# Blockwise inverses of unit triangular matrices: the step from 16 to 32 rows in compact 32x32 squares

## The chip, the cores and the metric

The kernel runs on one NeuronCore of a Trainium2 chip. The core has a matrix engine (TensorE, "PE" in the profile, with its weight loads as "PEld"), a vector engine (VectorE, "DVE"), a scalar engine (ScalarE, "ACT"), a general engine (GpSimd, "POOL"), and a queue engine that issues most of the transfers (SyncE, "SP"). Matrix products read their operands from the on-chip memory SBUF, which has 128 partitions, and write to eight PSUM banks of 128 partitions by 512 f32 columns. The metric is the device time of one execution in microseconds, taken as the median of several runs. The profile is one further execution with the hardware profiler on.

## The reference

The reference computes two layers of a hybrid decoder for 256 tokens of width 2048, all in f32. Each layer is a token mixer followed by a SwiGLU block, with adaptive modulation and layer norms around both. The mixer of the first layer has a group of mLSTM heads and a group of 16 RWKV-7 heads; the mixer of the second has retention heads and eight gated DeltaNet heads. Two of these hold a linear recurrence with a rank-one correction:

```python
# RWKV-7, per head, one token at a time
sa = jnp.einsum('bhij,bhj->bhi', S, at)
S = S * wt[:, :, None, :] + sa[..., None] * bt[:, :, None, :] + vt[..., None] * kt[:, :, None, :]
# gated DeltaNet, per head and chunk
ut = jnp.eye(CHUNK) + jnp.where(strict, jnp.einsum('cbhtd,cbhsd->cbhts', kb, kc) * gamma, 0.0)
u = lax.linalg.triangular_solve(ut, vc * bc[..., None], left_side=True, lower=True)
```

The kernel treats both with chunks of 128 tokens: inside a chunk the corrections of all tokens follow from one triangular system, a unit triangular matrix of 128 by 128 per head and chunk. The kernel forms the inverse of that matrix and multiplies with it.

## The kernel before

The 256 tokens are two tiles of 128 partitions (NT = 2). Every large weight product is computed in a split form: the f32 weights stream in from memory, ScalarE rounds them to a "hi" part and VectorE subtracts to get the "lo" part (`split`, L750 and L751), and TensorE adds three products per block into a PSUM bank of the group "g" (`part`, L765 to L767: hi times hi, lo times hi, hi times lo). All small products of the mixers go to banks of the groups "m" (three banks) and "c" (two banks), as full f32 products. VectorE also computes the modulation rows (L686), one long instruction for each 128 columns.

The small work of the mixers is not a stage of its own: it is woven into the stream of weight products. The order on every engine is written out by a planner (class `Plan`). The program is first built once, the planner simulates all engines with a table of costs (`cost`, `matmul`, the constants `MARGINS`, `LAND`, `CROSS`, `RATE`), and it picks, on each engine, the ready instruction with the lowest priority number. The priority is the program's order plus a shift that the table `PLACES` gives for each range of instruction numbers. It also decides which buffer each tile gets. The program is then built a second time with that order imposed on each engine.

`inverses(mt, dd)` receives eight triangular matrices `mt` (four heads, two chunks) in one tile and a tile `dd` of the same size for the result. It is called six times: four times by `rwkv_heads` (one call for each batch of four heads) and twice by `gdn_group`. It works in four steps, each closing with a `yield`.

1. Diagonal blocks of 16 rows. L1048 to L1058 cut the 16x16 blocks out into a compact tile `e` (8 matrices by 16 columns) and run a recurrence of fourteen steps on VectorE, each a lane shuffle, a product and an addition. L1060 spreads the result over the full width of 128 columns with a mask of blocks (`blk`), which gives `dt`; L1064 transposes each 128x128 matrix on TensorE and L1065 copies the result to `d`. So `d` and `dt` hold the block-diagonal inverse and its transpose, with zeros elsewhere.
2. From 16 to 32 rows. L1074 multiplies the full 128x128 `mt` with every second block of columns of `d` (64 columns), L1078 masks the result to the wanted blocks (`lev`), L1081 multiplies with `dt`, L1084 adds into `d`, L1088 transposes again and L1089 copies to `dt`.
3. From 32 to 64 rows. L1097 multiplies 32x32 squares (for the two pairs of squares, each in a bank of its own), L1099 copies out, L1103 and L1105 give the new square and its transpose, L1108 and L1109 put them into `d` and `dt`.
4. From 64 to 128 rows. L1116 to L1125 do the same with 64x64 squares; only the transpose `dt` is made.

The result `dt` then goes into the products of the heads (for RWKV L1312, for DeltaNet L1710). GpSimd runs the triangular masks (L1131), the scalings for the decay weights (L1532, L1675) and a few memsets (L1330).

Of the kernel before, what the change touches and what calls it, by code (L numbers as in the profile page):

```python
# [16 lines left out]
ALU = mybir.AluOpType  # L17
# [4 lines left out]
P = 128  # L22
# [34 lines left out]
for _name, _w in [("ident", 128), ("cum", P + 1), ("tr", 128), ("ones", 128), ("sl", 128), ("tri", 32), ("diag", 16), ("blk", 8),  # L57
                  ("lev", 64), ("bones", 128), ("hsel", 2), ("freq", 64)]:
    CONS[_name] = (_n, _w)
    _n += _w  # L60
# [3 lines left out]
def constants():  # L64
# [3 lines left out]
    def put(name, a):  # L68
        o, w = CONS[name]
        c[:, o:o + w] = a  # L70
# [11 lines left out]
    put("blk", u // BASE == np.arange(P // BASE)[None])  # L82
    j = np.arange(64)
    s = j // BASE * 2 * BASE + j % BASE
    put("lev", (u // (2 * BASE) == s[None] // (2 * BASE)) & (u % (2 * BASE) >= BASE))
# [108 lines left out]
def finish(g):  # L194
# [10 lines left out]
MARGINS = {'Activation': 0.9875423830141832, 'DVE': 1.0101153058187327, 'PE': 1.014122181386299, 'Pool': 1.1973257770806474}  # L205
LAND, CROSS, RATE, SOON = 2471.8499431610267, 67.12701229691764, 396.01772112428813, 250.0
PLACES = (
# [29 lines left out]
class Plan:  # L237
# [85 lines left out]
    def cost(self, i):  # L323
# [26 lines left out]
        if e == "Pool":  # L350
            d = {"TensorScalarAffineSelect": 1100 if n == 512 else 900, "TensorTensor": 950, "TensorScalarPtr": 1200, "Memset": 610}.get(op, 100)
            return d, d
# [206 lines left out]
class Trunk:  # L559
# [475 lines left out]
    def inverses(self, mt, dd):  # L1035
# [4 lines left out]
        d, dt = dd[:, 0], dd[:, 1]  # L1040
        halves = [slice(0, 4), slice(4, 8)]
        four = lambda x: x.rearrange("p (h t) -> p h t", h=4)
# [16 lines left out]
        for hs in halves:  # L1059
            v.tensor_tensor(dt[:, hs, :].rearrange("p h (n c) -> p h n c", c=BASE), e[:, hs, :].unsqueeze(2).to_broadcast([P, 4, 8, BASE]),  # L1060
                            self.con("blk").unsqueeze(1).unsqueeze(3).to_broadcast([P, 4, 8, BASE]), ALU.mult)
            b = self.bank()
            for j in range(4):
                nc.tensor.transpose(b[:, P * j:P * j + P], dt[:, hs.start + j, :], self.ident)  # L1064
            nc.scalar.activation(d[:, hs, :], four(b[:]), AF.Copy)  # L1065
        yield
        mm = nc.tensor.matmul
        mask = self.con("lev").unsqueeze(1).to_broadcast([P, 4, 64])
        dv = d.rearrange("p h (n two b) -> p h n two b", two=2, b=BASE)
        b, p = [], []  # L1070
        for hs in halves:
            x = self.bank()
            for j in range(4):
                mm(x[:, 64 * j:64 * j + 64], mt[:, hs.start + j, :], dv[:, hs.start + j, :, 0, :], start=True, stop=True)  # L1074
            b.append(x)
        for x in b:
            p.append(self.own([P, 4, 64], "P", 2))
            v.tensor_tensor(p[-1][:], four(x[:, 0:256]), mask, ALU.mult)  # L1078
        for hs, x, y in zip(halves, b, p):
            for j in range(4):  # L1080
                mm(x[:, 256 + 64 * j:320 + 64 * j], dt[:, hs.start + j, :], y[:, j, :], start=True, stop=True)  # L1081
        for hs, x in zip(halves, b):
            o = dv[:, hs, :, 0, :]
            v.tensor_tensor(o, x[:, 256:512].rearrange("p (h n b) -> p h n b", h=4, b=BASE), o, ALU.add)  # L1084
        for hs in halves:
            x = self.bank()
            for j in range(4):
                nc.tensor.transpose(x[:, P * j:P * j + P], d[:, hs.start + j, :], self.ident)  # L1088
            nc.scalar.activation(dt[:, hs, :], four(x[:]), AF.Copy)  # L1089
# [3 lines left out]
        b = [self.bank(), self.bank()]  # L1093
        y = self.own([P, 8, 32], "P", 2)
        for h in range(8):
            for x, (ev, od) in zip(b, pairs):
                mm(x[od, 32 * h:32 * h + 32], mt[ev, h, od], d[ev, h, ev], start=True, stop=True)  # L1097
        for x, (ev, od) in zip(b, pairs):
            nc.scalar.activation(y[od], x[od, 0:256].rearrange("p (h b) -> p h b", h=8), AF.Copy)  # L1099
        for h in range(8):  # L1100
            c = slice(256 + 32 * h, 288 + 32 * h)
            for x, (ev, od) in zip(b, pairs):
                mm(x[od, c], dt[od, h, od], y[od, h, :], start=True, stop=True)  # L1103
            for x, (ev, od) in zip(b, pairs):
                mm(x[ev, c], y[od, h, :], dt[od, h, od], start=True, stop=True)  # L1105
# [882 lines left out]
```

## Time and profile before

| what | value |
|---|---|
| median of 3 runs | 2699.81 us (2694.32 to 2701.47) |
| the profiled execution | 2710.22 us, its span 2708.5 us |
| mean granted TensorE clock | 0.984 of full speed |
| TensorE busy | 2616.7 us, 97% of the span |
| VectorE busy | 2003.0 us, 74% |
| ScalarE busy | 1270.1 us, 47% |
| GpSimd busy | 87.1 us, 3% |
| instructions in the profile | 33578 |

A share of busy time is an average over stages with different limits, so the table only says where to look. In this profile the RWKV and mLSTM work of the first layer lies between about 125 and 700 us, the first SwiGLU block between about 700 and 1420 us, the DeltaNet groups between about 1420 and 1740 us, retention and the second output product up to about 2000 us, and the second SwiGLU block after that. A row that begins with a time is a single block of instructions in order of time; a row with "x" and a mean is a group over the whole span. The duration of one TensorE instruction contains its way through the array, which overlaps with the next instruction, so the distance between two starts, not the duration, is what it costs in a full queue.

### The profile page before, as it was taken

To read this page: it belongs to the slowest core of one execution; us is meant where nothing else is said; L and a number is where in the kernel's file an instruction comes from. 1 tells how busy PE (TensorE), PEld (TensorE's weight loads), DVE (VectorE), ACT (ScalarE), POOL (GpSimd) and SP (SyncE) were. 2 spreads that over 40 slices of the span, in tenths; PEclk is the share of its full clock that TensorE was granted. 3 is DMA by queue.
4 is the path that set the end of the run, shared out by engine and by line. 5 is a ranking of instruction groups with operands and counts; after the bars stand their busy time and mean duration, and the time that the engine had idled before them with its cause. 6 is when DMAs were issued, how large, how long until landed. Compare 5 with 4: busy or idle time off the path is not lost.

```text
span 2708.5 us, 33578 instructions
## 1 busy us (share of the span) xinstructions
PE 2616.7 (97%) x12906; PEld 2157.6 (80%) x12906; DVE 2003.0 (74%) x3153; ACT 1270.1 (47%) x1705; POOL 87.1 (3%) x88
## 2 busy tenths in 40 slices
PE   4799999999999999999999999999999999999997
PEld 2578877888788888888888887888788888888886
DVE  7998877888777677767778998876956664456457
ACT  2464545565644444434446654444554444443442
POOL 0000000100000000000001102000000000000000
PEclk9899998999999999999999999999999999999999
DMA  9966655665688888867856866765657775556554
GB/s 396 386 251 236 238 202 204 239 231 192 221 310 309 321 313 322 310 218 295 325 210 213 309 234 235 267 249 205 241 210 275 257 286 191 194 200 228 187 188 169
DMA packets 105659, 681.60 MB, mean 252 GB/s; under 512 B 11861, under 2 KB 15129, under 8 KB 27417
## 3 DMA queue, kind: packets, MB, share of 16 engines
q1 hardware_dynamic: 104346, 677.36, 68.3%
q8 instruction: 101, 1.65, 0.2%
q10 hardware_dynamic: 1152, 2.10, 0.2%
q14 instruction: 60, 0.49, 0.1%
HBM read 668.89 MB, written 10.52 MB: 251 GB/s over the span
## 4 chain that ended last, share of the span: by engine, by line
PE 86%; DVE 7%; DMA 4%; ACT 1%; issue 1%; POOL 0%; SPq 0%; DVEq 0%; ACTq 0%
PE g L765 26%; PE g L766 26%; PE g L767 26%; DMA raw<-ada 2%; DVE lo L751 1%; DMA a<-ada 1%; DMA y<-w_ab 1%; PE m L1010 1%; DVE raw L686 1%; ACT hi L750 1%; PE m L1290 0%; PE m L1312 0%; PE c L1468 0%; PE m L1308 0%; PE m L1321 0%
## 5 line engine op out<-in xcount | busy, mean ns | idle before, releaser
L751 DVE TENSOR_TENSOR lo<-raw,hi 128x1024 fp32r<-128x1024 f32 (+2 forms) x802 | 970.0, 1213 | 567.7 <-ACT hi L750 564.6
L750 ACT ACTIVATE hi<-raw 128x1024 fp32r<-128x1024 f32 (+2 forms) x802 | 842.6, 1053 | 1083.9 <-PE g L767 1027.0
L765 PE MATMUL g<-hi,h 128*128 128x512 f32 (+2 forms) x2312 | 901.7, 392 | 13.5 <-ACT h L829 13.1
L766 PE MATMUL g<-lo,h 128*128 128x512 f32 (+2 forms) x2312 | 902.4, 391 | 0.6 <-DVE lo L751 0.5
L767 PE MATMUL g<-hi,h 128*128 128x512 f32 (+2 forms) x2312 | 900.6, 391 | 0.0
L765 PEld LDWEIGHTS g<-hi,h 128*128 128x128 f32 x2312 | 436.0, 189 | 103.1 <-ACT h L829 14.0
L766 PEld LDWEIGHTS g<-lo,h 128*128 128x128 f32 x2312 | 436.5, 189 | 89.3 <-DVE lo L751 2.7
L767 PEld LDWEIGHTS g<-hi,h 128*128 128x128 f32 x2312 | 436.5, 189 | 88.7 <-issue 4.2
L765 PE MATMUL g<-hi,a 128*128 128x512 f32 x920 | 358.7, 392 | 0.5 <-DVE t L906 0.5
L767 PE MATMUL g<-hi,a 128*128 128x512 f32 x920 | 358.3, 390 | 0.0
L766 PE MATMUL g<-lo,a 128*128 128x512 f32 x920 | 358.2, 390 | 0.0
L765 PEld LDWEIGHTS g<-hi,a 128*128 128x128 f32 x920 | 172.4, 188 | 37.5 <-DVE t L906 1.0
L767 PEld LDWEIGHTS g<-hi,a 128*128 128x128 f32 x920 | 172.8, 188 | 35.6
L766 PEld LDWEIGHTS g<-lo,a 128*128 128x128 f32 x920 | 172.8, 188 | 35.5
L686 DVE SCALAR_TENSOR_TENSOR raw<-raw,silu_c 128x2048 f32<-128x2048 f32 x82 | 188.6, 2303 | 11.1 <-DMA raw<-ada 6.7
L686 DVE SCALAR_TENSOR_TENSOR za<-za,silu_c 128x2048 f32<-128x2048 f32 x56 | 127.9, 2284 | 1.4 <-DMA za<-ada 1.4
L686 DVE SCALAR_TENSOR_TENSOR zt<-zt,silu_c 128x2048 f32<-128x2048 f32 x38 | 86.8, 2285 | 2.1 <-DMA zt<-ada 2.1
L1675 POOL TENSOR_SCALAR s<-cons_sb,log_alpha 128x128 f32<-128x128 f32 x16 | 28.7, 1806 | 997.0 <-DVE log_alpha L1619 853.9
L1474 DVE SCALAR_TENSOR_TENSOR f<-c,cols_sb,f 128x253 f32<-128x253 f32 (+2 forms) x120 | 55.9, 477 | 4.9 <-ACT f L1471 4.1
L948 ACT ACTIVATE t<-m,affine 128x128 f32<-128x128 f32 x96 | 35.6, 467 | 4.4 <-PE m L945 2.5
L686 DVE SCALAR_TENSOR_TENSOR a<-a,silu_c 128x2048 f32<-128x2048 f32 x16 | 36.1, 2288 | 1.9 <-DMA a<-ada 1.9
L765 PE MATMUL m<-hi,h 128*128 128x512 f32 x24 | 11.2, 468 | 23.6 <-ACT h L829 23.6
(481 smaller groups left out, 2137.7 us busy)
## 6 DMA issues: line engine op xcount, KB each, us to landing
raw<-gu SPq DMA_DIRECT2D x176, 1024.0 KB, 4.8
raw<-dn SPq DMA_DIRECT2D x88, 1024.0 KB, 4.8
raw<-ada SPq DMA_DIRECT2D x82, 1024.0 KB, 5.2
raw<-w_cd SPq DMA_DIRECT2D x60, 1024.0 KB, 4.9
za<-ada SPq DMA_DIRECT2D x56, 1024.0 KB, 7.0
raw<-w_ab SPq DMA_DIRECT2D x48, 1024.0 KB, 5.1
zt<-ada SPq DMA_DIRECT2D x38, 1024.0 KB, 7.0
a<-ada SPq DMA_DIRECT2D x16, 1024.0 KB, 16.4
```

What stands on the lines that cost most here:

```text
L686: v.scalar_tensor_tensor(w[:], w[:], 1.0, self.sc[:], ALU.mult, ALU.mult, accum_out=m[:, i:i + 1])
L750: nc.scalar.activation(hi[:, :2 * n], ws, AF.Copy)
L751: nc.vector.tensor_tensor(lo[:, :2 * n], ws, hi[:, :2 * n], ALU.subtract)
L765: mm(o, ah, wh, start=start and k == 0, stop=False)
L766: mm(o, ah, wl, start=False, stop=False)
L767: mm(o, al, wh, start=False, stop=stop and k == 3)
L948: nc.scalar.activation(h32[:, j, :], b[:, P * j:P * j + P], AF.Identity, bias=self.ab[:, sub + 1, 16 + k:17 + k], scale=self.ab[:, sub + 1 ...
L1010: nc.tensor.transpose(b[:, P * k:P * k + P], gs[:, t, P * k:P * k + P], self.ident)
L1474: v.scalar_tensor_tensor(o[:, d:T], b[:, T * j:T * j + T - d], self.col(wname, 4 * (tile0 + i + j) + 3 - d), o[:, d:T], ALU.mult, ALU.add)
L1675: nc.gpsimd.tensor_scalar(L[:], sl, self.gl[:, t, 4 * g + j:4 * g + j + 1], None, ALU.mult)
```

## The change

Step 1 no longer spreads the blocks of 16 rows over 128 columns and no longer transposes on TensorE. The two blocks of each 32x32 square are put side by side in a compact tile `a` (8 matrices by 32 columns), with a mask `par` that says which of the two blocks a partition belongs to. VectorE's square transpose, which transposes each 32x32 square of its operand by itself, gives its counterpart `c`.

Step 2 works on the four diagonal 32x32 squares of each matrix: 32 products of 32x32 by 16 columns, one scalar-tensor-tensor on VectorE that masks and adds the identity part (`two`), 32 products of 32x32 by 32 columns, a copy by ScalarE, and a second square transpose by VectorE. ScalarE and VectorE place the squares into `dt` (two squares each); `d` now has only 64 columns per matrix and keeps its squares compact. GpSimd clears `dt` and `d` at the start, since they are no longer written in full.

Step 3 uses one bank for both pairs of squares, and the square that no later step reads (the one of the second pair in `d`) is no longer computed. Step 4 is unchanged but for the narrower `d`.

The constants `blk` and `lev` go, `par` and `two` come. In the planner the cost of a GpSimd memset now grows with its size, the constants are fitted anew, and the table of shifts is a new one for the changed program.

```diff
-for _name, _w in [... ("tri", 32), ("diag", 16), ("blk", 8),
-                  ("lev", 64), ("bones", 128), ("hsel", 2), ("freq", 64)]:
+for _name, _w in [... ("tri", 32), ("diag", 16), ("par", 2),
+                  ("two", 32), ("bones", 128), ("hsel", 2), ("freq", 64)]:
...
+    put("par", u % 32 // BASE == np.arange(2)[None])
+    put("two", u % 32 == c32)
...
-MARGINS = {'Activation': 0.9875423830141832, 'DVE': 1.0101153058187327, 'PE': 1.014122181386299, 'Pool': 1.1973257770806474}
-LAND, CROSS, RATE, SOON = 2471.8499431610267, 67.12701229691764, 396.01772112428813, 250.0
+MARGINS = {'Activation': 0.9876056006034423, 'DVE': 1.0058989261580051, 'PE': 1.014, 'Pool': 1.2193352478552955}
+LAND, CROSS, RATE, SOON = 2470.0, 66.83757847790392, 395.92384460318044, 250.0
 PLACES = (
...
-        d, dt = dd[:, 0], dd[:, 1]
+        room = dd[:].rearrange("p a h t -> p (a h t)")
+        eight = lambda x: x.rearrange("p (h t) -> p h t", h=8)
+        dt, d, yi, a = eight(room[:, 0:1024]), eight(room[:, 1024:1536]), eight(room[:, 1536:1792]), eight(room[:, 1792:2048])
...
+        nc.gpsimd.memset(room[:, 0:1536], 0.0)
+        nc.scalar.activation(yi[:, :, BASE:], two[:, BASE:].unsqueeze(1).to_broadcast([P, 8, BASE]), AF.Copy)
...
-        for hs in halves:
-            v.tensor_tensor(dt[:, hs, :]..., e[:, hs, :]..., self.con("blk")..., ALU.mult)
-            b = self.bank()
-            for j in range(4):
-                nc.tensor.transpose(b[:, P * j:P * j + P], dt[:, hs.start + j, :], self.ident)
-            nc.scalar.activation(d[:, hs, :], four(b[:]), AF.Copy)
+        v.tensor_tensor(a.rearrange("p h (n c) -> p h n c", n=2), e[:].unsqueeze(2).to_broadcast([P, 8, 2, BASE]),
+                        par.unsqueeze(1).unsqueeze(3).to_broadcast([P, 8, 2, BASE]), ALU.mult)
+        c = self.own([P, 8, 32], "P", 2)
+        v.transpose(c[:], a)
         yield
...
+        quarters = [slice(32 * q, 32 * q + 32) for q in range(4)]
+        x = self.bank()
+        for h in range(8):
+            for r in quarters:
+                mm(x[r, BASE * h:BASE * h + BASE], mt[r, h, r], c[r, h, 0:BASE], start=True, stop=True)
+        v.scalar_tensor_tensor(yi[:, :, 0:BASE], eight(x[:, 0:8 * BASE]), par[:, 1:2], two[:, 0:BASE].unsqueeze(1).to_broadcast([P, 8, BASE]),
+                               ALU.mult, ALU.add)
+        for h in range(8):
+            for r in quarters:
+                mm(x[r, T + 32 * h:T + 32 * h + 32], yi[r, h, :], a[r, h, :], start=True, stop=True)
+        z = eight(x[:, T:2 * T])
+        c = self.own([P, 8, 32], "P", 2)
+        nc.scalar.activation(c[:], z, AF.Copy)
+        v.transpose(d[:, :, 0:32], c[:])
+        for q in (1, 3, 0, 2):
+            r = quarters[q]
+            if q % 2:
+                nc.scalar.activation(dt[r, :, r], z[r], AF.Copy)
+            else:
+                v.tensor_copy(dt[r, :, r], c[r])
+        v.tensor_copy(d[32:64, :, 32:64], d[32:64, :, 0:32])
         yield
...
-        b = [self.bank(), self.bank()]
+        x = self.bank()
...
-            for x, (ev, od) in zip(b, pairs):
-                mm(x[od, c], dt[od, h, od], y[od, h, :], start=True, stop=True)
+            for ev, od in pairs[:1]:
+                mm(x[od, o], dt[od, h, od], y[od, h, :], start=True, stop=True)
...
-            v.tensor_copy(d[od, :, ev], z[od])
+        for ev, od in pairs[:1]:
+            v.tensor_copy(d[od, :, 0:32], eight(x[od, T:2 * T]))
```

More of the change, by code (lines that the diff above doesn't have):

```diff
@@ L56 @@
 _n = 0
-for _name, _w in [("ident", 128), ("cum", P + 1), ("tr", 128), ("ones", 128), ("sl", 128), ("tri", 32), ("diag", 16), ("blk", 8),
-                  ("lev", 64), ("bones", 128), ("hsel", 2), ("freq", 64)]:
+for _name, _w in [("ident", 128), ("cum", P + 1), ("tr", 128), ("ones", 128), ("sl", 128), ("tri", 32), ("diag", 16), ("par", 2),
+                  ("two", 32), ("bones", 128), ("hsel", 2), ("freq", 64)]:
     CONS[_name] = (_n, _w)
@@ L81, in constants @@
     put("diag", u % BASE == c16)
[L82 to L85, printed above, removed]
+    put("par", u % 32 // BASE == np.arange(2)[None])
+    put("two", u % 32 == c32)
     put("bones", u // 64 == t // 64)
@@ L350, in cost @@
         if e == "Pool":
-            d = {"TensorScalarAffineSelect": 1100 if n == 512 else 900, "TensorTensor": 950, "TensorScalarPtr": 1200, "Memset": 610}.get(op, 100)
+            d = {"TensorScalarAffineSelect": 1100 if n == 512 else 900, "TensorTensor": 950, "TensorScalarPtr": 1200, "Memset": 610 + 0.5 * n if n > 256 else 610}.get(op, 100)
             return d, d
@@ L1039, in inverses @@
         nc, v = self.nc, self.nc.vector
-        d, dt = dd[:, 0], dd[:, 1]
+        room = dd[:].rearrange("p a h t -> p (a h t)")
+        eight = lambda x: x.rearrange("p (h t) -> p h t", h=8)
+        dt, d, yi, a = eight(room[:, 0:1024]), eight(room[:, 1024:1536]), eight(room[:, 1536:1792]), eight(room[:, 1792:2048])
         halves = [slice(0, 4), slice(4, 8)]
+        par, two = self.con("par"), self.con("two")
+        nc.gpsimd.memset(room[:, 0:1536], 0.0)
+        nc.scalar.activation(yi[:, :, BASE:], two[:, BASE:].unsqueeze(1).to_broadcast([P, 8, BASE]), AF.Copy)
         four = lambda x: x.rearrange("p (h t) -> p h t", h=4)
@@ L1058, in inverses @@
                 v.tensor_tensor(e[:, :, k + 1:], e[:, :, k + 1:], x, ALU.add)
-        for hs in halves:
-            v.tensor_tensor(dt[:, hs, :].rearrange("p h (n c) -> p h n c", c=BASE), e[:, hs, :].unsqueeze(2).to_broadcast([P, 4, 8, BASE]),
-                            self.con("blk").unsqueeze(1).unsqueeze(3).to_broadcast([P, 4, 8, BASE]), ALU.mult)
-            b = self.bank()
-            for j in range(4):
-                nc.tensor.transpose(b[:, P * j:P * j + P], dt[:, hs.start + j, :], self.ident)
-            nc.scalar.activation(d[:, hs, :], four(b[:]), AF.Copy)
+        v.tensor_tensor(a.rearrange("p h (n c) -> p h n c", n=2), e[:].unsqueeze(2).to_broadcast([P, 8, 2, BASE]),
+                        par.unsqueeze(1).unsqueeze(3).to_broadcast([P, 8, 2, BASE]), ALU.mult)
@@ L1066, in inverses @@
+        c = self.own([P, 8, 32], "P", 2)
+        v.transpose(c[:], a)
         yield
         mm = nc.tensor.matmul
[L1068 to L1089, printed above, removed]
+        quarters = [slice(32 * q, 32 * q + 32) for q in range(4)]
[3 more added lines that the diff above has]
+                mm(x[r, BASE * h:BASE * h + BASE], mt[r, h, r], c[r, h, 0:BASE], start=True, stop=True)
@@ L1095, in inverses @@
         for h in range(8):
-            for x, (ev, od) in zip(b, pairs):
-                mm(x[od, 32 * h:32 * h + 32], mt[ev, h, od], d[ev, h, ev], start=True, stop=True)
-        for x, (ev, od) in zip(b, pairs):
-            nc.scalar.activation(y[od], x[od, 0:256].rearrange("p (h b) -> p h b", h=8), AF.Copy)
+            for ev, od in pairs:
+                mm(x[od, 32 * h:32 * h + 32], mt[ev, h, od], d[ev, h, 0:32], start=True, stop=True)
+        for ev, od in pairs:
+            nc.scalar.activation(y[od], eight(x[od, 0:T]), AF.Copy)
@@ L1100, in inverses @@
         for h in range(8):
[L1101 to L1105, printed above, removed]
-        for x, (ev, od) in zip(b, pairs):
-            z = x[:, 256:512].rearrange("p (h b) -> p h b", h=8)
-            v.tensor_copy(d[od, :, ev], z[od])
-            nc.scalar.activation(dt[ev, :, od], z[ev], AF.Copy)
+            o = slice(T + 32 * h, T + 32 * h + 32)
@@ L1110, in inverses @@
+            for ev, od in pairs[:1]:
+                mm(x[od, o], dt[od, h, od], y[od, h, :], start=True, stop=True)
+            for ev, od in pairs:
+                mm(x[ev, o], y[od, h, :], dt[od, h, od], start=True, stop=True)
+        for ev, od in pairs[:1]:
+            v.tensor_copy(d[od, :, 0:32], eight(x[od, T:2 * T]))
+        for ev, od in pairs:
+            nc.scalar.activation(dt[ev, :, od], eight(x[ev, T:2 * T]), AF.Copy)
         yield
@@ L1115, in inverses @@
             for j in range(4):
-                mm(x[64:, 64 * j:64 * j + 64], mt[:64, hs.start + j, 64:], d[:64, hs.start + j, :64], start=True, stop=True)
+                mm(x[64:, 64 * j:64 * j + 64], mt[:64, hs.start + j, 64:], d[:64, hs.start + j, :], start=True, stop=True)
             b.append(x)
```

50 rows, old and new, of the table PLACES are left out of this document.

## The prediction

> **What bounds the kernel now.** I read the profile's first page before anything else, for the busy shares, the granted clock and the shares of the chain that ended last.
>
> ```profile
> span 2708.5 us, 33578 instructions
> PE 2616.7 (97%) x12906; PEld 2157.6 (80%) x12906; DVE 2003.0 (74%) x3153; ACT 1270.1 (47%) x1705; POOL 87.1 (3%) x88
> ...
> PEclk9899998999999999999999999999999999999999
> ...
> PE 86%; DVE 7%; DMA 4%; ACT 1%; issue 1%; POOL 0%; SPq 0%; DVEq 0%; ACTq 0%
> ```
>
> TensorE is busy 97% of the span and is 86% of the chain. Next comes the table of stretches, cut at the stages; its columns are the stretch, its length, then the busy time (and instructions) of PE, weight loads, VectorE, ScalarE and GpSimd, the granted clock, and the DMA share. The four inverses of the RWKV heads lie in the first row, the two of the DeltaNet groups in the third.
>
> ```profile
> 125.00:700.00 575.00, 564.92 (x3250) 459.36 (x3249) 482.33 (x1112) 318.49 (x550) 41.48 (x47) 0.96 0.63 227
> 700.00:1420.00 720.00, 719.83 (x3225) 595.11 (x3224) 519.32 (x541) 313.22 (x334) 0.00 (x0) 1.00 0.77 287
> 1420.00:1740.00 320.00, 314.40 (x1894) 265.10 (x1893) 281.47 (x598) 176.34 (x289) 38.54 (x28) 1.00 0.68 250
> ```
>
> In both mixer stages TensorE idles under 2% (10.1 of 575 us, 5.6 of 320 us), because weight products fill the gaps between the small steps. VectorE has 93 us and 39 us to spare there, and ScalarE more. So a microsecond of TensorE work taken out of an inverse should come off the time, and a shorter latency of the same inverse should not, except through the few waits left. The list of waits for the inverse's late steps confirms that these waits are small (us in total, times, longest):
>
> ```profile
> PE m L1116 <- DVE a L1108: 0.6, 2, 0.4
> PE m L1123 <- ACT P L1120: 0.6, 2, 0.3
> ```
>
> **What is removed on TensorE.** The chain of waits (start, us, what) through the second inverse gives each block's share of the path, free of the overlap that the instruction times contain. An f32 product leaves two records, so x16 is eight products; a transpose leaves one, so x4 is four.
>
> ```profile
> 314.53 0.44 PE m L1064 x4
> ...
> 315.20 0.44 PE m L1064 x4
> ...
> 315.87 1.78 PE m L1074 x16
> ...
> 319.50 0.84 PE m L1081 x8
> ...
> 321.09 0.84 PE m L1081 x8
> 321.93 0.44 PE m L1088 x4
> ...
> 325.31 0.44 PE m L1088 x4
> 325.74 0.62 PE m L1097 x32
> ...
> 328.39 0.43 PE g L767
> 328.81 0.23 PE g L765
> ```
>
> The two rounds of eight transposes (L1064, L1088) cost 4 x 0.44 = 1.76 us, the two rounds of eight 128-row products (L1074, L1081) 1.78 + 2 x 0.84 = 3.46 us. Together 5.22 us per inverse, 31.3 us for six.
>
> **What is added on TensorE.** Two rounds of 32 products of 32 rows by 32 columns (moving width 16, then 32), eight heads in four squares on the diagonal. The trace of before has no round on four diagonal squares, so I bound it by its neighbours, from the order in time of TensorE. The first three rows are the block of L1103 and L1105 that alternates over four squares; the last two are a block on one square (its partner had no bank yet).
>
> ```profile
> 327.56 0.22 PE L1103 MATMUL m<-P,y 32*32 32x32 f32 x2
> ...
> 328.20 0.19 PE L1105 MATMUL m<-y,P 32*32 32x32 f32 x1
> 328.32 0.50 PE L767 MATMUL g<-hi,h 128*128 128x512 f32 x1
> ...
> 235.29 0.69 PE L1097 MATMUL m<-y,a 32*32 32x32 f32 x16
> 235.91 0.49 PE L765 MATMUL g<-hi,h 128*128 128x512 f32 x1
> ```
>
> Four squares: 32 products (64 records) from 327.56 to 328.32, 0.76 us. One square: eight products from 235.29 to 235.91, 0.62 us, up to 78 ns each. Two squares (the L1097 x32 row above): 16 in 0.62 us. So the time goes with the products per square, eight in all three, and four squares overlap. The new rounds also have eight per square, so I take 0.76 us for each; the width of 16 may save a little, which I leave out. The return to full-size products costs 0.43 - 0.23 = 0.20 us (L767 against L765). Each round is 0.96 us, the pair 1.92 us. If nothing overlapped, a round would be 4 x 0.62 = 2.48 us, plus 0.20: the upper bound, 5.36 us for the pair. The lower bound is a pair without the return cost, 1.52 us.
>
> A rule speaks against the lower price. The Trainium skill, page "TensorE: Matmul & The Clock Gate", section "Wait — 56ns, not 53.3ns?", says that matmul starts are never closer than about 25 ns, however narrow the operand. By it 64 records would take 1.6 us, and the estimated gain of six inverses would be 6 x (5.22 - 3.6) = 9.7 us. The trace disagrees: 64 records start within 0.76 us, 12 ns apart.
>
> **The third step** (blocks of 32 into 64) loses the eight products of L1103 for the second pair. They ran beside the others at eight per square, so they are worth nothing by the same rule of rows. But it now uses one PSUM bank for both pairs, so a pair can't be held back for a bank as at 235.29 in the first inverse, where the two pairs ran one after the other. Merged, one round of 0.62 us and its return of 0.20 us go away there, and about as much in L1103/L1105; I take 1.1 us for the whole kernel, between 0 and 1.6.
>
> **TensorE in sum:** 6 x (5.22 - 1.92) + 1.1 = 20.9 us less.
>
> **The other engines.** Groups by line, shape kept apart (busy us, mean ns), and for the start of the recurrence and the first use of the result the summary of one line (min/median/max ns, first and last start):
>
> ```profile
> L1078 DVE TENSOR_TENSOR P<-m,cons_sb 128x256 f32<-128x256 f32 x12 | 4.6, 413 | 0.0
> L1056 DVE STREAM_SHUFFLE e<-e 128x112 f32<-128x112 f32 x6 | 1.8, 297 | 0.0
> L1685 DVE SCALAR_TENSOR_TENSOR a<-m,v,t 128x128 f32<-128x128 f32 x16 | 4.8, 341 | 0.1
> L1108 DVE COPY y<-m 32x256 f32<-32x256 f32 x8 | 3.4, 424 | 2.2 <-issue 2.0
> L1065 ACT ACTIVATE y<-m 128x512 f32<-128x512 f32 x8 | 4.6, 595 | 7.3 <-PE m L1064 7.2
> L1099 ACT ACTIVATE P<-m 32x256 f32<-32x256 f32 x12 | 4.5, 377 | 0.4 <-PE m L1097 0.2
> L1330 POOL MEMSET s<- 128x256 f32 x4 | 1.2, 312 | 24.5 <-DVE e L1058 14.1 <-DVE e L1056 10.4
> ...
> L1048 DVE TENSOR_TENSOR s<-a,cons_sb x24: 402/417/1301, 182.3 to 1676.7; 32x256 f32<-32x256 f32 x24
> L1060 DVE TENSOR_TENSOR y<-e,cons_sb x8: 681/684/689, 222.6 to 505.7; 128x512 f32<-128x512 f32 x8
> ```
>
> VectorE loses two masks of 512 columns (2 x 0.684), two of 256 (2 x 0.413), two additions of 256 (the same size, 2 x 0.413) and one copy (0.424): 3.44 us. It gains one mask of 256 (0.413), one scalar-tensor-tensor of 128 (0.341), three copies of 256 columns (at most 0.424 each, 1.27) and two square transposes of 256 columns. The trace has no such transpose. The shuffle is the nearest row, since it too moves lanes: 0.297 us for 112 columns, so between 0.41 (a plain 256-column pass) and 0.68 (the shuffle scaled by columns). I take 0.45, near the plain pass. Sum 2.92, a saving of 0.5 us per inverse; at 0.68 it is nothing. ScalarE loses four copies of 512 columns (2.38 us) and gains four of at most 0.377 (1.51). Neither engine sets the end, so I count zero; what hides them is the full TensorE queue. Without that cover they would still be a small gain.
>
> GpSimd gets a memset of 1536 columns. From 0.312 us at 256 columns, 1.9 us at most by scaling. It stands ahead of the recurrence, whose first instruction starts at 182.3 us while the result is first used at 222.6: some 40 us hide it. Behind it in GpSimd's queue stand the triangular masks of the heads and the scalings for the mLSTM weights; GpSimd is busy 3% of the span. The tile it clears must now be free 40 us earlier than before; the two earlier tiles of that pool belong to a batch that is finished by then. Zero.
>
> **The sum.** The profiled execution took 2710.2 us (span 2708.5 and 1.7 around it); on it the change gives 2710.2 - 20.9 = 2689. That execution lies 10.4 us above the median of 2699.8, so against the median I expect 2699.8 - 20.9 = **2679 us**. The new shifts reorder everything, and I put no gain or loss of their own in the sum. About 0.3%, 8 us, is what a measurement here can tell from no change.
>
> **Rivals.** The first is the granted clock. Rows of the table of stretches around the second and third inverse (seventh number after the length: the clock):
>
> ```profile
> 332.30:335.72 3.42, 3.42 (x38) 3.09 (x38) 3.35 (x6) 2.52 (x7) 0.00 (x0) 1.00 0.22 53
> 335.72:339.13 3.41, 3.41 (x16) 3.15 (x16) 1.61 (x7) 0.60 (x2) 0.00 (x0) 0.55 0.73 293
> ...
> 345.96:349.37 3.41, 3.41 (x17) 3.19 (x15) 0.42 (x1) 0.62 (x2) 0.00 (x0) 0.50 0.62 262
> 349.37:352.78 3.41, 3.41 (x21) 2.56 (x20) 0.42 (x1) 1.06 (x4) 0.00 (x0) 0.95 0.00 0
> ```
>
> Right after the small products the clock falls to a half from about 336 to 349.5 us, though the queue is full. At half clock, 14 us do the work of 7, so such a stretch costs some 7 us. (a) **Slower:** the two new rounds use small corners of the array and call up one more such stretch behind each of the six inverses: 6 x 7 = 42 us, against a gain of 21, gives 2721. It decides from the third new stretch on, and from the fifth the kernel is slower by more than 0.3%. Against it: 0.76 us is short, and full products stand on both sides. (b) **Faster still:** the new order loses two such stretches, 14 us: 2665. The same page of the Trainium skill, section "HAM oscillation — how this bites in real kernels", puts the fall down to idle gaps over about 3.4 us. By that (a) can't happen. The trace disagrees here: TensorE is busy 3.42 of 3.42 us in the stretch just before the fall.
>
> (c) **The squares don't overlap:** the upper bound of 5.36 us per pair leaves 6 x (5.22 - 5.36) + 1.1 = 0.3 us: 2700, no change. For it only that products of one square don't overlap; against it the four-square block. (d) **The freed time isn't filled:** the chain through VectorE takes over the mixer stages and products come late. Then half or all of the gain is lost: 2690 to 2700. For it VectorE's 84% and 88%; against it TensorE's 15.7 us of idle time in both stages. (e) **The change doesn't do what it says:** the order searched anew is worse elsewhere. If the 15.7 us double and one half-clock stretch of 7 us is added, 2679 + 23 = 2702; the order can also be better and save about half of the idle time: 2671.
>
> **How the numbers follow.** Forecast 0.47 (own range 2670 to 2688); (a) 0.06; (b) 0.15; (c) 0.07; (d) 0.13; (e) worse 0.06, better 0.06. Faster by over 0.3% (below 2692): 0.47 + 0.15 + 0.06 + 0.05 of (d) = 0.73. Slower by over 0.3% (above 2708): (a) and somewhat under half of (e) for orders worse than priced, 0.09. The rest, 0.18, is no change. The range runs from 2660, below (b), to 2703, past (e); outside lie (a) and the tails, under 0.2.
>
> **What would show it.** Right: TensorE shows 6 x (-16 - 32 + 128 - 16) = 384 more records (16 transposes and 16 products removed, 64 small products added and 8 removed per inverse), yet its busy time falls by about 21 us; the new rounds take 0.7 to 0.8 us with heads and squares alternating; TensorE's idle share stays at 3%. Wrong: rounds of over 1.5 us (c); more idle time ahead of products, put down to VectorE (d); more or fewer rows at clock 0.5 between 125 and 700 us (a, b); a gain in stages without inverses (e).

## The result and the profile after

The changed kernel takes **2675.12 us** (median of 4 runs, 2674.08 to 2677.11) against 2700.64 us of the kernel before on the same chip (4 runs, 2694.32 to 2705.73). The ratio is 0.9908, with a 95% interval of 0.9886 to 0.9929: about 25 us, or 0.9%, faster. The prediction was 2679 us. Its profiled execution took 2674.08 us, that of before 2710.22 us, and these 36 us are more than the medians differ by. The reason is the granted clock, as will be seen.

First the page of the changed kernel: the span, the busy shares, the clock in 40 slices, and the shares of the chain that ended last.

```profile
span 2672.3 us, 34350 instructions
...
PE 2580.0 (97%) x13290; PEld 2114.3 (79%) x13290; DVE 1992.2 (75%) x3153; ACT 1264.4 (47%) x1705; POOL 96.0 (4%) x94
...
PEclk9899999999999999999999999999999999999999
...
PE 81%; DVE 11%; DMA 4%; issue 2%; ACT 1%; POOL 0%; SPq 0%; DVEq 0%; POOLq 0%; ACTq 0%
```

TensorE has 13290 records, 384 more than before, and is busy 36.7 us less. It is still the bound at 97%. Next the table of stretches of the changed kernel, for the two mixer stages with inverses (columns as in the prediction: the stretch, its length, PE, weight loads, VectorE, ScalarE, GpSimd, then the granted clock, the DMA share and GB/s).

```profile
125.00:700.00 575.00, 563.70 (x3646) 448.53 (x3645) 491.52 (x1153) 331.58 (x580) 48.67 (x51) 1.00 0.65 236
...
1420.00:1740.00 320.00, 315.92 (x2058) 264.54 (x2057) 285.73 (x578) 173.32 (x274) 38.55 (x30) 0.99 0.71 264
```

TensorE idles 11.3 and 4.1 us there, 15.4 together, against 15.7 before: in these stages the freed time was filled. In the first SwiGLU block, between 700 and 1420 us, TensorE is busy 717.83 of 720 us where it was busy 719.83 before; a wait of 2.2 us for ScalarE is new there. And the clock of the first stretch went from 0.96 to 1.00. The order in time of TensorE around the new rounds of the first inverse (start, duration, line, operands, and x records):

```profile
226.88 0.39 PE L765 MATMUL g<-hi,h 128*128 128x512 f32 x1
227.19 0.73 PE L1072 MATMUL m<-P,a 32*32 32x16 f32 x64
227.85 0.50 PE L763 MATMUL g<-hi,h 128*128 128x512 f32 x1
228.19 0.39 PE L764 MATMUL g<-lo,h 128*128 128x512 f32 x1
...
231.29 0.75 PE L1077 MATMUL m<-y 32*32 32x32 f32 x64
231.98 0.50 PE L763 MATMUL g<-hi,h 128*128 128x512 f32 x1
...
233.44 0.69 PE L1096 MATMUL m<-y,a 32*32 32x32 f32 x32
234.06 0.50 PE L765 MATMUL g<-hi,h 128*128 128x512 f32 x1
```

A new round of 32 products takes 0.66 us to the next weight product with 16 columns, 0.69 us with 32. A weight product follows another after 0.23 us in this stream; the one before the round takes 0.31 and the one behind it 0.34, so a round costs 0.66 + 0.08 + 0.11 = 0.85 us in all. Step 3 (L1096) now stands in one block of 0.62 us also in this first inverse, where before the two pairs stood apart. The other new instructions, in the summaries of their lines (min/median/max ns, first and last start, form):

```profile
L1065 DVE STREAM_TRANSPOSE P<-y x4: 441/444/457, 226.4 to 486.1; 128x256 f32<-128x256 f32 x4
...
L1081 DVE STREAM_TRANSPOSE y<-P x4: 440/442/448, 232.9 to 494.2; 128x256 f32<-128x256 f32 x4
...
L1043 POOL MEMSET y<- x4: 1377/1381/1384, 124.1 to 455.3; 128x1536 f32 x4
```

The square transposes take 0.44 us, the memset 1.38 us. Two rows of the changed kernel's list of waits belong to the memset (who waited for whom: us in total, times, longest us):

```profile
POOL y L1043 <- PE m L1311: 54.8, 2, 52.8
...
POOL y L1043 <- DVE q L749: 42.7, 1, 42.7
```

It waits up to 52.8 us for products of an earlier batch, and once 42.7 us for VectorE, before it can clear its tile.

**Where the rest of the 36 us is.** In both kernels TensorE runs at half clock in a few stretches, and these can be cut out. Rows of the table of stretches, first of the kernel before:

```profile
271.20:278.00 6.80, 6.80 (x18) 4.48 (x17) 2.80 (x5) 2.60 (x9) 3.12 (x2) 0.50 0.47 157
336.10:349.70 13.60, 13.60 (x60) 12.93 (x59) 6.60 (x13) 2.29 (x5) 0.00 (x0) 0.50 0.60 223
431.60:448.70 17.10, 17.10 (x70) 15.45 (x69) 6.17 (x10) 7.44 (x14) 0.00 (x0) 0.50 0.43 157
479.40:482.80 3.40, 3.40 (x12) 2.73 (x11) 2.47 (x13) 1.48 (x2) 2.77 (x4) 0.50 1.04 351
1960.80:1964.20 3.40, 3.40 (x11) 2.73 (x11) 3.30 (x11) 1.91 (x5) 0.00 (x0) 0.50 0.83 277
```

and of the kernel after:

```profile
1408.80:1412.20 3.40, 3.40 (x16) 2.92 (x14) 1.21 (x2) 2.38 (x6) 0.00 (x0) 0.50 0.84 188
1490.70:1494.10 3.40, 3.40 (x18) 3.36 (x18) 3.22 (x12) 1.83 (x4) 0.00 (x0) 0.50 0.62 204
```

Before: 44.3 us, with TensorE busy in all of it, so 22.2 us are lost. After: 6.8 us, 3.4 lost, none of it between 125 and 700 us. (Two parts are left out: the first 125 us, where half clock takes some 31 us before and 34 after but TensorE is idle for nearly half of the time, and the last 12 us, where TensorE does nothing.) Without these losses the spans are 2708.5 - 22.2 = 2686.3 and 2672.3 - 3.4 = 2668.9. So some 17 us of this pair come from the operations and 19 from the clock. The experiments test both halves.

### The profile page after: what moved, and what is told of

It is laid out like the page before. It is cut to its first block, busy times and chain, and to the rows that moved or that the text cites. A ratio compares the mean times of both kernels' runs of the same rounds, so it can differ in the third digit from the quotient of the medians.

```text
span 2672.3 us, 34350 instructions
## 1 busy us (share of the span) xinstructions
PE 2580.0 (97%) x13290; PEld 2114.3 (79%) x13290; DVE 1992.2 (75%) x3153; ACT 1264.4 (47%) x1705; POOL 96.0 (4%) x94
## 4 chain that ended last, share of the span: by engine, by line
PE 81%; DVE 11%; DMA 4%; issue 2%; ACT 1%; POOL 0%; SPq 0%; DVEq 0%; POOLq 0%; ACTq 0%
PE g L764 25%; PE g L765 25%; PE g L763 25%; DVE lo L749 3%; DVE raw L684 1%; DMA raw<-ada 1%; PE m L1008 1%; DMA a<-ada 1%; DMA t<-xt 1%; DVE f L1473 1%; DMA y<-w_ab 1%; DMA y<-w_low 1%; PE m L1289 1%; DVE za L684 1%; ACT hi L748 0%
## 5 line engine op out<-in xcount | busy, mean ns | idle before, releaser
L1130 POOL TENSOR_SCALAR_AFFINE_SELECT a<-a 128x512 f32<-128x512 f32 (+1 forms) x20 | 25.7, 1294 | 159.6 <-ACT a L1291 139.9
```

The source lines that it names most:

```text
L1130: self.nc.gpsimd.affine_select(x, x, pattern=[[0, n] for n in dims] + [[1, P]], compare_op=ALU.is_gt if strict else ALU.is_ge, fill=0.0, b ...
```

## The experiments

Two theories stand against each other. A: the gain is the TensorE work that went away, at the prediction's prices. B: the new order carries it, by its shifts or by the clock that it happens to meet. Where instructions are added, they are put into the planned order directly behind the one they follow, so that everything else keeps its order.

**Both kernels once more**, unchanged.

> The kernel before, unchanged, to see how its time goes with its mean granted clock from run to run. Theory A (TensorE's work sets the gain, about 21 us of it): the times lie within 2694 to 2710 us, a lower clock goes with a longer time, and even the runs with the best clock (0.989 or so, as the changed kernel has) stay 15 us or more above the changed kernel's 2675. Theory B (most of the gain is the new order, which keeps the clock at full speed in the RWKV stage): runs with a clock of 0.989 come down to about 2680, and the profile shows the half-clock stretches behind the second and third inverse again.

> The changed kernel, unchanged, beside the others on the same chip. Both theories: 2675 us within 3 us, a ratio of 0.991 to the kernel before.

Before: 2700.34 us (12 runs, 2691.62 to 2710.9). After: 2675.74 us (4 runs, 2674.03 to 2678.14), ratio 0.9889, interval 0.9854 to 0.9924. The profiled execution of before now has these stretches at half clock and no others behind the head:

```profile
423.40:437.10 13.70, 13.70 (x54) 12.05 (x54) 5.20 (x10) 7.13 (x13) 0.00 (x0) 0.50 0.44 160
1949.20:1952.60 3.40, 3.40 (x11) 2.71 (x12) 3.30 (x10) 1.84 (x5) 0.00 (x0) 0.50 0.87 282
```

That is 17.1 us, 8.6 lost; its span of 2696.9 less 8.6 is 2688.3, within 2 us of the 2686.3 above, though the two executions lie 12 us apart. The stretch behind the second inverse isn't there this time, in the same order of instructions. So the kernel before varies because the same program meets half clock for 17 us in one execution and 44 in another. Over the 82 runs of it beside the experiments the median is 2703.0 us (2690.4 to 2718.0), and the time follows the mean clock: nine runs at 0.992 have a median of 2692.6, thirteen at 0.984 one of 2710.1. (One run, 2694.8 us at 0.953, falls out of this.) After, repeated, has three stretches of 3.4 us, one of them at 665.8 us, 5.1 lost, and 2673.4 - 5.1 = 2668.3.

The clock alone doesn't make the gain, as A has it: at 0.989 or 0.990, which the changed kernel has too, the kernel before takes 2693.7 to 2701.6 us (12 runs), and its fastest run of all is 12 us above the slowest of the changed kernel.

**The new rounds twice.** Each of the twelve new rounds is issued a second time, directly behind the first. (`self.more` is true in the second build alone, and `self.extra` names the added instructions.)

```diff
...
+        for again in range(2 if self.more else 1):
+            for h in range(8):
+                for r in quarters:
+                    i = mm(x[r, BASE * h:BASE * h + BASE], mt[r, h, r], c[r, h, 0:BASE], start=True, stop=True)
+                    if again:
+                        self.extra.add(i.ins.name)
...
+        for again in range(2 if self.more else 1):
+            for h in range(8):
+                for r in quarters:
+                    i = mm(x[r, T + 32 * h:T + 32 * h + 32], yi[r, h, :], a[r, h, :], start=True, stop=True)
+                    if again:
+                        self.extra.add(i.ins.name)
```

> The changed kernel with both new rounds of 32 products issued twice (the second time right behind the first, same operands, same result; the order of all other instructions is kept). Theory A: the second copy needs no change of form, 32 products on four squares take about 0.55 us, so 12 x 0.55 = 6.6 us more than the changed kernel. If products started no closer than 25 ns, 64 records would take 1.6 us: 12 x 1.6 = 19 us more. If nothing overlapped over the squares (4 x 0.52 us): 25 us more. Theory B: under 3 us more, since TensorE's work is not what the gain came from.

2692.97 us (9 runs, 2690.59 to 2699.66), ratio 0.9959 (0.9939 to 0.9978): 17.2 us more than the changed kernel, near the figure of the 25-ns rule. The trace shows that it isn't by that rule. The order in time of TensorE in the doubled kernel, in the first and the second inverse:

```profile
227.59 1.26 PE L1074 MATMUL m<-P,a 32*32 32x16 f32 x128
228.78 0.50 PE L764 MATMUL g<-hi,h 128*128 128x512 f32 x1
...
322.89 1.10 PE L1082 MATMUL m<-y 32*32 32x32 f32 x106
327.24 0.54 PE L1082 MATMUL m<-y 32*32 32x32 f32 x22 [3.25 <-issue]
```

and its TensorE waits (us in total, times, longest us):

```profile
PE m L1082 <- issue: 7.7, 5, 3.2
...
PE m L1074 <- issue: 1.9, 1, 1.9
...
PE m L1111 <- issue: 1.5, 1, 1.5
```

128 records take 1.19 us, 0.53 more than 64: 12 x 0.53 = 6.4 us, as A has it. The other 11.1 us are idle time of a kind that the changed kernel's list of TensorE waits doesn't have among its longest rows: in the middle of a doubled block (L1074, L1082), or soon after it (L1111), TensorE stops for up to 3.25 us, waiting for nothing that the profile shows. 6.4 + 11.1 = 17.5, against 17.2 measured. That the two agree is partly chance, since the sum leaves out the clock: the doubled kernel has 17.0 us at half clock behind the head, and 6.8 of them set in during the stop of 3.25 us. Without the 8.5 us lost there, its span of 2689.8 would be 2681.3, some 12 to 13 us above the 2668.9 and 2668.3 of after. So not all of the 17.5 us comes through, and about 4 us of the difference is the clock.

**The same, set apart.** The second copy comes four TensorE products later, so each copy is a block of 64 records again.

```diff
-            m += follow.get(i, [])
+            if i in follow:
+                due.append((n + APART, follow[i]))
+            while due and due[0][0] <= n:
+                m += due.pop(0)[1]
...
+APART = 4
```

> As the doubled rounds, but the second copy of each round stands four TensorE products (about 0.9 us of full-size ones) behind the first and writes to a free part of the bank. Theory C (the doubled rounds cost 17 us instead of 6.6 because 256 instructions within 1.2 us outrun TensorE's supply of instructions, which shows as idle time put down to nothing): the idle time put down to issue on these rounds goes, and each copy costs a round with its change of form, 12 x 0.85 = 10 us: about 2686. Theory D (a second round costs 1.4 us wherever it stands): 17 us again, 2693.

2690.64 us (4 runs, 2688.3 to 2693.09), ratio 0.9937 (0.9924 to 0.9951): 14.9 us more than after. The TensorE waits of this kernel:

```profile
PE m L1084 <- issue: 3.5, 2, 2.4
...
PE m L1075 <- issue: 0.8, 1, 0.8
```

The work at the full price of a round is 12 x 0.85 = 10.2 us, the idle time in these rows 4.3; together 14.5 of the 14.9. Setting the copies apart took away more than half of the idle time put down to issue. So the density of the small instructions has to do with the stops, but four products between the blocks weren't enough to end them, and why TensorE stops there isn't shown. Here too the sum leaves out the clock: 20.4 us at half clock, 10.2 lost, so 2691.4 - 10.2 = 2681.2, the same as in the doubled kernel. At full clock, then, setting the copies apart gained nothing in these two executions, and the median lies between C's 2686 and D's 2693; neither is borne out.

**The old TensorE work put back.** Behind the second new round stand again 16 transposes and 16 full products, with their results unused.

```diff
+        if self.more:
+            for i in range(16):
+                self.extra.add(nc.tensor.transpose(x[:, 0:P], mt[:, i % 8, :], self.ident).ins.name)
+            for i in range(16):
+                self.extra.add(mm(x[:, P:P + 64], mt[:, i % 8, :], mt[:, i % 8, 0:64], start=True, stop=True).ins.name)
```

> The changed kernel with the removed TensorE work put back and nothing else: behind the second new round of each inverse, 16 transposes of 128x128 and 16 products of 128 rows by 64 columns into a free part of the same bank, results unused, the order of all other instructions kept. Theory A: 6 x 5.22 = 31 us more than the changed kernel, about 2706. Theory B: under 15 us more, since the order and its clock are kept.

2701.95 us (10 runs, 2698.49 to 2705.57), ratio 0.9993 (0.9972 to 1.0013): 26.2 us more than after, where A expected 31 and B under 15. The chain of waits of this kernel in the first inverse (start, us, what):

```profile
231.72 0.68 PE m L1078 x50
232.40 1.90 PE m L1081 x16
234.30 3.52 PE m L1083 x32
237.82 0.29 PE g L764
```

The work put back takes 5.42 us per inverse, 32.5 for six (5.22 in the prediction's rows). It has three stretches of half clock of 3.4 us, as the repeated kernel after, so its span of 2701.5 against 2673.4 compares directly: 28.1 of 32.5 us. So TensorE work in these places counts at 86% (81% by the medians). Most of the rest went into idle time: between 125 and 1740 us TensorE idles 13.9 us in this kernel, against 17.6 and 17.4 in the two executions of after. The copy on ScalarE waits for the added work too, so the inverse also comes later, but no idle time of TensorE comes of it. B falls as the whole cause.

One more row of this kernel, from its table of stretches, matters for the next experiment:

```profile
125.00:700.00 575.00, 565.45 (x3755) 454.42 (x3753) 483.22 (x1140) 320.58 (x565) 43.76 (x51) 1.00 0.64 231
```

**The kernel before, filled.** If B's clock has a cause in the order of TensorE, it must be found there. The order in time of the kernel before, just ahead of its half-clock stretch that begins at 336.1 us:

```profile
331.78 0.40 PE L766 MATMUL g<-lo,h 128*128 128x512 f32 x1
332.19 0.68 PE L1116 MATMUL m<-y,a 64*64 64x64 f32 x8
332.86 0.67 PE L1123 MATMUL m<-y,P 64*64 64x64 f32 x8
...
335.80 1.75 PE L1312 MATMUL m<-s,y 128*128 128x64 f32 x8
...
337.73 0.77 PE L767 MATMUL g<-hi,h 128*128 128x512 f32 x1
```

For 5.5 us, 3.9 of them ahead of the fall, only products of 2 to 64 columns stand there, none of 512. In the changed kernel the same steps are broken up, and no half clock follows:

```profile
328.63 1.14 PE L1115 MATMUL m<-y,a 64*64 64x64 f32 x16
...
332.27 0.48 PE L765 MATMUL g<-hi,h 128*128 128x512 f32 x1
332.59 1.01 PE L1311 MATMUL m<-s,y 128*128 128x64 f32 x8
333.41 0.48 PE L763 MATMUL g<-hi,h 128*128 128x512 f32 x1
```

So in the kernel before, each RWKV inverse gets eight products of 512 columns behind its last round of 64x64 squares. Their results are unused; they are only work, 32 x 0.23 = 7.4 us.

```diff
+        if self.more:
+            for i in range(8):
+                k = 2 * (i % 2)
+                self.extra.add(mm(yb[:], self.dense[:, 0, i % 4, 0:P], self.dense[:, 0, k:k + 2, :].rearrange("p k t -> p (k t)"), start=True, stop=True).ins.name)
```

> The kernel before, with eight full-size products (128 rows by 512 columns, hi parts of the activations, results overwritten) put into TensorE's order behind the last 64x64 product of each of the four RWKV inverses, the order of the rest kept: 4 x 8 x 0.23 = 7.4 us of added work. Theory B2 (the half-clock stretches of the kernel before come from runs of several us of small f32 products without a full-size one between them, and cost about 10 us on average over its runs): the stretches go, the clock is 0.991 or better in nearly all runs, the spread of the times shrinks from 20 us to under 8, and the median is no higher than the kernel before, 2695 to 2703. Theory A2 (the stretches have nothing to do with what stands between): 7 us more, 2710, with the same spread of clocks.

2699.65 us (6 runs, 2697.51 to 2702.69) against 2707.37 for before on that chip (16 runs), ratio 0.997 (0.9959 to 0.9982): **with 7.4 us more work it is 7.7 us faster** (3.3 us against the median of the 82 runs), and it varies by 5 us where before varies by over 20. All six runs have a mean clock of 0.990 to 0.992; the runs of before go down to 0.981. The table of stretches of the filled kernel:

```profile
125.00:700.00 575.00, 564.02 (x3331) 456.68 (x3330) 489.79 (x1139) 325.39 (x566) 42.35 (x47) 1.00 0.63 230
```

The clock there is 1.00, as in the changed kernel; TensorE's idle time, 11.0 us, isn't less than before (10.1). No stretch at half clock is left between the head and the tail. The span of 2695.8 less 7.4 is 2688.4: a third figure for the kernel before at full clock, beside 2686.3 and 2688.3. The Trainium skill, page "TensorE: Matmul & The Clock Gate", section "HAM oscillation — how this bites in real kernels", puts the falls of the clock down to idle gaps. At 336.1 us the trace disagrees: TensorE has no idle gap in the 3.9 us ahead. Elsewhere it agrees in kind: in the changed kernel, the stretch at 1408.8 us sets in as TensorE comes out of 2.17 us of idle time, and in the doubled kernel the one at 325.9 us sets in during a stop of 3.25 us.

So the added products keep the clock up, but what starts a stretch at half clock stays open. B2's runs of small products aren't enough for it. In the kernel with the old work put back, each of the six inverses has 6 to 7 us of transposes and products of at most 128 columns between two full-size ones (231.72 to 237.82 us in the rows above), and no half clock follows any of them. They aren't needed for it either: ahead of the stretches of before at 271.2 and 479.4 us stand products of 256 and 512 columns, with idle gaps of 0.81 and 1.24 us among them. These two are gone in the filled kernel as well.

**Both kernels without shifts.** The table is emptied, so both get the plain priority order.

```diff
-PLACES = (
-    (0, 240), (16, 0), (18, 920), ...
-)
+PLACES = ()
```

> The kernel before with an empty table of shifts (the planner's order by program order alone). Both theories: slower than the kernel before; by how much says what the searched shifts are worth there. I expect 2730 to 2790.

> The changed kernel with an empty table of shifts. Theory A (the operations alone are worth some 17 us, the rest of the gain of 26 is the order): 12 to 22 us faster than the kernel before with an empty table. Theory B (most of the gain is the new shifts): less than 8 us faster than it.

2734.71 us (4 runs, 2733.5 to 2736.52; ratio 1.0101, 1.0086 to 1.0116) and 2703.91 us (10 runs, 2700.17 to 2707.48; ratio 0.9986, 0.9968 to 1.0004). The shifts are worth 27 us to the one on that chip (32 against the median of the 82 runs) and 28 to the other; without any, the change still brings 30.8 us, more than A's 12 to 22, and the shifts fall as what carries it. The excess is the clock again: behind the head, half clock takes 44.2 us of the one profiled execution and 27.2 of the other. At full clock they stand at 2732.6 - 22.1 = 2710.5 and 2702.3 - 13.6 = 2688.7, which is 21.8 us apart and inside A's range.

**One bank and two banks in step 3.** The kernel before gets one bank for both pairs of squares, the changed one gets two.

```diff
-        b = [self.bank(), self.bank()]
+        b = [self.bank()] * 2
```

```diff
-        x = self.bank()
+        b = [self.bank(), self.bank()]
...
-            for ev, od in pairs:
+            for x, (ev, od) in zip(b, pairs):
```

> The kernel before with the third step (32 to 64 rows) in one PSUM bank for both pairs instead of two; nothing else, the same number of instructions and the same shifts. My prediction gave this part 1.1 us, between 0 and 1.6. Against the mean over the clock states of the kernel before (2690 to 2718) that is hardly to be seen; what can be seen is whether the order that follows from it changes the half-clock stretches.

> The changed kernel with the third step in two banks again; the same number of instructions and the same shifts. By my prediction 1.1 us slower (0 to 1.6), so 2676 to 2678; if the single bank is what freed the other small work from waiting for banks, 5 us or more.

2714.63 us (6 runs, 2708.47 to 2715.59) against 2697.27 for before there, ratio 1.0048 (1.002 to 1.0076), and 2695.85 us (10 runs, 2690.08 to 2702.42), ratio 0.9998 (0.998 to 1.0016). Both got slower by 17 to 20 us. One edit gives a bank and the other takes one, so this isn't simply the bank's price. In both, TensorE idles more in the two mixer stages: 23.0 us where the kernel before idles 15.7, and 25.6 where the changed kernel idles 15.4. The likely reading is that each table of shifts was found for one program, and that a planner with one buffer more or less turns the same shifts into another order; it wasn't tested apart. What the bank itself is worth stays open.

**Old shifts in the stage between.** The new table has no shift in the first SwiGLU block. The kernel after gets those of before there, moved by 100 instructions; in the second version some further into the DeltaNet stage too.

```diff
-    ..., (4532, 560), (4535, 0), (9468, 40), ...
+    ..., (4532, 560), (4535, 0), (4764, -960), (5096, 0), (5208, 1240), ..., (9463, 0), (9468, 40), ...
```

> The changed kernel with one part of its shift table replaced: in the first SwiGLU block, up to the second norm, where the new table has no shifts at all, it gets the shifts that the kernel before has for the same instructions (there are 100 instructions more ahead of them, and the shifts are moved by that). The stage from the first norm to the DeltaNet groups took 3.7 us more in the changed kernel than in the filled kernel before. If that loss lies in the missing shifts (E), the stage gets some 3 us shorter and the median goes from 2675.7 to about 2673 or less. If a shift is worth something only in the program and order that it was searched in (F), as the two kernels with one bank altered suggest, the median stays or rises: 2675 to 2690.

> As the kernel with the old shifts in the first SwiGLU block, with the old shifts also kept over the first instructions of the DeltaNet groups in place of three of the new ones. By E about 2673, by F 2675 to 2695, above the other one since more of the new table is lost.

2676.51 us (6 runs, 2674.99 to 2680.19; ratio 0.9912, 0.9888 to 0.9937) and 2677.06 us (6 runs, 2674.12 to 2679.87; ratio 0.9915, 0.9889 to 0.9942): no difference from the kernel after, within its spread. E falls, and the shifts of that block are worth nothing here.

## Why the prediction was right

The time came out 4 us below the forecast, inside its own range, and mainly for the reason given. That it came so close is partly luck: the sum took 2 us too much from the operations and nothing from the clock, which gave 9, and it started from a median 3 us below that of the 82 runs. Point by point:

- **TensorE work taken out comes off the time.** Right, at 86% (28.1 of 32.5 us put back; 26.2 by the medians).
- **Removed, 5.22 us per inverse.** Near enough: 5.42 when put back in one block.
- **Added, 0.96 us per round.** 0.85 with 16 columns, 0.88 with 32: the four squares overlap, in rounds of 0.66 to 0.69 us. Rival (c), at up to 2.48, falls. So does the price by the 25-ns rule of the Trainium skill (page "TensorE: Matmul & The Clock Gate", section "Wait — 56ns, not 53.3ns?"): 64 records in 0.66 us are 10 ns apart, 128 in 1.19 us 9 ns. The width of 16 does save a little, 0.03 us.
- **Step 3, 1.1 us.** The round that stood in two parts stands in one, as said. That the second part waited for a bank is the prediction's reading, and no row of the waits shows it. The worth of the step was not measured alone, since both kernels with the bank changed got slower in other places too.
- **VectorE and ScalarE, counted at nothing.** The transpose was taken at 0.45 us and measures 0.44. ScalarE's busy time falls by 5.7 us; six times the predicted 0.87 is 5.2.
- **GpSimd, at nothing.** Right in the price, 1.38 us against at most 1.9. The reason for the tile was wrong: an earlier batch does hold it, up to 52.8 us. It starts late without harm: no row of TensorE's longest waits leads back to it.
- **The sum, 20.9 us.** At full clock the three figures for before (2686.3, 2688.3, 2688.4) and the two for after (2668.9, 2668.3) lie 17.4 to 20.1 apart, about 19. With the rounds at their measured price the sum would have been 6 x (5.22 - 1.73) + 1.1 = 22.0, some 3 us more than came off. About 1 of these is idle time: between 125 and 1740 us TensorE idles 15.9 and 16.8 us in the two executions of before, 17.6 and 17.4 in those of after. Where the other 2 are isn't traced.
- **Rival (d), the freed time isn't filled.** Falls for the mixers: 15.4 us idle against 15.7. In the first SwiGLU block 2.0 us of idle time are new.
- **Rival (a), new stretches at half clock.** Falls: no half clock follows a new round. Between 125 and 700 us the first execution of after has none and the second one stretch of 3.4 us, at 665.8, long after the last RWKV inverse.
- **Rival (b), stretches lost.** This is the step that failed: the sum counted the clock at nothing, and (b) had 0.15. It came true beside the forecast. The kernel before loses to the clock its median of 2703.0 less (2687.7 + 1.7) = 13.6 us, with 2687.7 the mean of its three figures and 1.7 the time around the span; after, with a median of 2675.1 over its eight runs, loses 2675.1 - (2668.6 + 1.7) = 4.8 us. So 9 us came from there (14 had been priced) and 19 from the operations; together they are the 28 us by which these medians differ.
- **Rival (e), the new shifts.** Falls as the cause: both kernels lose about as much without their shifts, and the gain is there without any. But the new shifts bear on the clock: without them the changed kernel has 27.2 us at half clock behind the head, with them 6.8 and 10.2.

The profiled execution lay 10.4 us above the median. The prediction carried this along as an offset; it was the clock, and had the half-clock stretches been cut out first, 2688 (2686.3 and 1.7 around it) would have stood where 2699.8 stood, with what the new order itself loses to the clock, some 5 us, still to be added.

## What to carry to other kernels

Cut the stretches at half clock out of both profiles before comparing them: executions of one kernel that lie 12 us apart then agree within 2. Where a kernel's time varies with its mean clock, look at what stands ahead of its stretches at half clock. Here the longest followed microseconds of small f32 products without a full-size one between, and full-size products put among them were worth more than the work they took; but not every such run is followed by half clock, so it has to be tried. And a table of priorities found by search may be worth something for its own program alone: leave it alone in an experiment, and add instructions behind fixed neighbours instead.

## What the runs showed that was not expected

Adding 32 products of 512 columns (7.4 us) made the old kernel 7.7 us faster, by keeping TensorE's clock at 1.00 from 125 to 700 us. And TensorE can stop within a block of small products: in blocks of 128 records (9 ns apart), it stood idle for up to 3.25 us after 106 of them, with nothing in the profile that it waited for. In the changed kernel, whose blocks of 64 stand farther apart, none of TensorE's longest waits is of this kind.
